# Seven-product down projection: splits of unsummed weight blocks first, two products exchanged, later transposes at a layer's end, three raw tiles before the mixer

## The chip, the cores and the metric

One core of a Trainium2 chip runs the whole program. The metric is the device time of one execution in microseconds (us), and smaller is better. TensorE is called PE here (its weight loads PEld), VectorE DVE, ScalarE ACT, GpSimd POOL, and the queue of SyncE that issues the loads of weights SP.

## The reference

Two residual layers over 256 positions and 2048 channels, all in fp32, end with an RMSNorm. Layer 0 mixes tokens with a convolution and pooling stage, layer 1 with a Fourier stage. Both layers then run the same two steps, which the change touches:

```python
x = x + square(relu(rms_norm(x) @ mlp_w1)) @ mlp_w2        # 2048 -> 8192 -> 2048
x = x + sigmoid(rms_norm(x) @ ple_w_gate) * (p @ ple_w_proj)  # 256 -> 2048
```

## The kernel before, in words

**Weights.** Every weight comes from HBM as a tile of 128 x 2048 fp32 (1 MB) into one of four `raw` buffers. Each is then split into a rounded part and a remainder, called high and low here, which go into the two halves of one of four `hl` buffers: ACT writes the high part (L110), DVE or POOL subtracts it from the raw tile to make the low part (L115). A product is three passes, high by high, high by low, low by high. `Weights.run_ahead` keeps the splits three tiles and the loads two further tiles ahead of the tile that PE takes next (`ws.next()`); a load is written down only while fewer than `RAW_BUFS` raw tiles are not yet used up.

**The mixer (`mlp`).** The 8192 hidden channels are 16 blocks of 512. `w1(q)` computes block q with four weight tiles, into two of the three PSUM buffers of `mm_pool`: first 16 matmuls with high weights (L591), then 16 narrower ones with low weights (L596). For each f from 0 to 7, `w2(f, n)` multiplies blocks 2f and 2f+1 by the weights of output columns n = 2 and n = 3 in the plain way (L356), 48 matmuls each. The columns n = 0 and 1 are computed in `pair(f)` with seven products where the plain way has eight: x is the weight tile of column block 0, y that of column block 1, each cut into halves of 1024 (at 0 and at q = 1024). Products 1, 2 and 3 take a half as it was loaded; 5, 4, 6 and 7 take sums of halves, which DVE adds in place into the raw tile (L107) before the half is split. A product is six matmuls (L668). Two such pairs of tiles, k = 0 and 1, make 14 products, and two products share one `hl` buffer, so a pair has seven such buffers, T0 to T6 below. The order of products is `SEVEN`. A prime marks a product of the second pair of tiles (4', 7').

**Gathers.** The products of a pair land in PSUM tiles a (products 1, 5), b (2, 3), c (7, 6), all from `mm_pool`, and d (4), from `sm_pool` with its two buffers. When the last product of a tile is written, `gather` adds the tile into `sums` or x on DVE (L655, L647, L649) and so frees it. After the last pair, `pair_end` combines the four parts of `sums` with x (L679).

**Order.** PE and SP run in the order in which the program is written. ACT and DVE are ordered at build time by a list scheduler that prefers what was written first; `tc.high_priority` moves work ahead. Each `tick()` counts one step of PE (six matmuls in a product), and `put_off` writes a piece of work down a number of ticks later.

**A layer's end.** When a column chunk of x is final, `Norm.chunk(c, steps)` squares it on ACT and, `steps` ticks later, transposes it on PE (eight transposes at L334 into two `sm_pool` tiles) and scales and splits it into `xT` (L273 on ACT, L278 on DVE). Chunk 2 is final before the last pair, chunks 0 and 1 after `pair_end`, chunk 3 after the last `w2`. Then `embed` computes four column blocks: a gate product with four weight tiles, one for each chunk of `xT` in the order 2, 0, 1, 3 (`ps_g`), a projection of the embedding p (`ps_e`, 12 matmuls), then sigmoid, product and sum. The embedding `pT` is loaded and split at the start of `embed`.

Of the kernel before, what the change touches and what calls it, by code (L numbers as in the profile page):

```python
# [26 lines left out]
LAYERS = 2  # L27
# [2 lines left out]
PRIO = 400  # L30
RAW_BUFS = 4

SEVEN = (1, 2, 5, 3, 6, 7, 4), (1, 5, 2, 6, 3, 4, 7)
RSQRT_MAGIC = float(0x5F3759DF)


# [8 lines left out]
class Weights:  # L45
# [4 lines left out]
    def __init__(self, nc, raw_pool, hl_pool, split_ahead, load_ahead):  # L50
        self.nc, self.raw_pool, self.hl_pool = nc, raw_pool, hl_pool
        self.split_ahead, self.load_ahead = split_ahead, load_ahead
        self.srcs, self.todo, self.raw, self.ready, self.last = [], [], {}, {}, {}
        self.loaded = self.split = self.used = 0
        self.hold = 10 ** 6

    def source(self, src, cols=2048, pieces=1):
        self.srcs.append((src, cols, pieces))
# [13 lines left out]
    def add_seven(self, tiles):  # L72

        q, parts = 1024, []
        for k, (x, y) in enumerate(tiles):
            x, y = self.source(x), self.source(y)
            made = {1: [("split", (x, 0))], 2: [("split", (x, q))], 3: [("split", (y, q))],
                    5: [("add", (x, 0), (y, 0)), ("split", (x, 0))],  # L80
                    6: [("add", (x, 0), (y, q)), ("split", (x, 0))],
                    7: [("add", (y, 0), (y, q)), ("split", (y, 0))],
                    4: [("add", (x, 0), (x, q)), ("split", (x, 0))]}
            parts += [made[p] for p in SEVEN[k]]
        for k in range(0, len(parts), 2):
            self.made([step + ((i * q, q) if step[0] == "split" else (q,))
                       for i, part in enumerate(parts[k:k + 2]) for step in part])

    def load(self, after_first=None):
        src, cols, pieces = self.srcs[self.loaded]  # L90
# [36 lines left out]
    def run_ahead(self):  # L127

        to_split = min(len(self.todo), self.used + 1 + self.split_ahead, self.hold)
        to_load = self.sources_of(min(len(self.todo), self.used + 1 + self.split_ahead + self.load_ahead) - 1)  # L130
        more = True
        while more:
            more = False
            if self.loaded < to_load and len(self.raw) < RAW_BUFS:
                self.load()
                more = True
            if self.split < to_split and self.loaded >= self.sources_of(self.split):
                self.divide()
                more = True
# [8 lines left out]
def encoder(ctx: ExitStack, tc: tile.TileContext, a, out: bass.AP):  # L148
# [60 lines left out]
    def add_ple(i):  # L209
        for n in range(4):  # L210
            parts = [(a["ple_w_gate"][i, n, c], 2048) for c in (2, 0, 1, 3)]
            parts.insert(0 if i == LAYERS - 1 and n == 3 else 4, (a["ple_w_proj"][i, n], 1024))
            for src, cols in parts:
                ws.add(src, cols=cols)

# [40 lines left out]
    def put_off(f, steps=4):  # L256

        later.append([steps, f])
# [11 lines left out]
    def divide_psum(dst, src, scale):  # L270

        hi, lo = dst
        nc.scalar.activation(hi, src, AF.Identity if scale is not None else AF.Copy,  # L273
                             scale=1.0 if scale is None else scale)
        if scale is None:
            nc.vector.tensor_tensor(lo, src, hi.bitcast(F32), ALU.subtract)
        else:
            nc.vector.scalar_tensor_tensor(lo, src, scale, hi.bitcast(F32), ALU.mult, ALU.subtract)  # L278
# [288 lines left out]
    def mlp(i, norm, after):  # L567
# [64 lines left out]
        def pair(f):  # L632


            tiles = {}

            def psum(p):

                key, half = {1: ("a", 0), 5: ("a", 1), 2: ("b", 0), 3: ("b", 1), 7: ("c", 0), 6: ("c", 1), 4: ("d", 0)}[p]
                if key not in tiles:  # L640
                    name = f"ps_s{i}_{f}{key}"
                    tiles[key] = sm_pool.tile([P, 512], F32, tag="sm", name=name) if key == "d" else psum_mm(name)
                return tiles[key][:, half * 512:(half + 1) * 512]

            def gather(p):
                if p == 3:
                    nc.vector.tensor_tensor(x[:, 0, :1024], tiles["b"], x[:, 0, :1024], ALU.add)  # L647
                elif p == 4:
                    nc.vector.tensor_tensor(x[:, 1, :512], tiles["d"], x[:, 1, :512], ALU.add)  # L649
                elif p in (5, 7):  # L650
                    ps, to = (tiles["a"], sums[:, :1024]) if p == 5 else (tiles["c"], sums[:, 1024:])
                    if f == 0:
                        nc.scalar.activation(to, ps, AF.Copy)
                    else:
                        nc.vector.tensor_tensor(to, ps, to, ALU.add)  # L655

            k = 0
            for q in (2 * f, 2 * f + 1):
                h, g = hidden[q], forms[q]
                for p in SEVEN[q % 2]:  # L660
                    if k % 2 == 0:
                        w = ws.next()
                    for kt in range(2):
                        for m, (s, j) in enumerate(PASSES_W_MOVES):
                            act = {1: h[:, s, kt, :P], 2: h[:, s, 2 + kt, :P], 4: h[:, s, 2 + kt, P:], 5: g[:, s, 0, kt],
                                   6: g[:, s, 1, kt], 7: g[:, s, 2, kt], 3: g[:, s, 3, kt]}[p]
                            col = (k % 2) * 1024 + kt * 512
                            nc.tensor.matmul(psum(p), lhsT=act, rhs=w[:, j, col:col + 512],  # L668
                                             start=q % 2 == 0 and kt == 0 and m == 0,
                                             stop=q % 2 == 1 and kt == 1 and m == 2)  # L670
                    tick()
                    k += 1
                    if q % 2:
                        gather(p)

        def pair_end():
            m1, m5, m7, m6 = (sums[:, k * 512:(k + 1) * 512] for k in range(4))
            c11, c12, c21, c22 = (x[:, t, n * 512:(n + 1) * 512] for t in range(2) for n in range(2))
            add, sub = ((lambda to, p, q, op=op: nc.vector.tensor_tensor(to, p, q, op)) for op in (ALU.add, ALU.subtract))  # L679
            add(c11, c11, m1)  # L680
            sub(m6, m6, m1)
            sub(c21, c21, m6)
            add(c21, c21, m7)
            after.chunk(0, 7)
            sub(m5, m6, m5)
            add(c12, c12, m5)
            add(c22, c22, m5)
            sub(c22, c22, m7)
            after.chunk(1, 9)

        put_off(scales, 10)
        w1(0)
        w1(1)
        for f in range(8):
            if f < 7:
                w1(2 * f + 2)
            w2(f, 2)
            if f < 7:
                w2(f, 3)
                pair(f)  # L700
                w1(2 * f + 3)
                continue
            after.chunk(2)
            pair(f)
            with tc.high_priority(offset=PRIO):
                pair_end()
            w2(f, 3)
            after.chunk(3)

    def embed(i, norm, after, gate_chunk=None, order=None):  # L710
        pt = work.tile([P, 2, S], F32, name="pt", tag="sv")
        nc.sync.dma_start(out=pt, in_=a["pT"][i])
        pT = act_pool.tile([P, 2, 2, S], F32R, tag="act", name=f"pT{i}")
        divide_psum(halves(pT), pt, None)
        for n in range(4):
            final = gate_chunk is not None and n == 3
            if final:
                pg = [psum_mm(f"ps_g{i}_{n}{k}") for k in range(3)]
                pe = [sm_pool.tile([P, 512], F32, tag="sm", name=f"ps_e{i}_{n}{t}") for t in range(2)]
                rows_product(pe, pT, range(2), True, True)  # L720
            else:
                pg = psum_mm(f"ps_g{i}_{n}")
                pe = psum_mm(f"ps_e{i}_{n}")
            if n == 3:
                ws.hold = ws.used + 7

# [22 lines left out]
            else:  # L749
                for k, c in enumerate((2, 0, 1, 3)):  # L750
                    rows_product(pg, norm.xT[c], range(4), k == 0, k == 3)
                rows_product(pe, pT, range(2), True, True)
                if order is not None and n == 3:
                    order.enter_context(in_order())
                for t in range(2):
# [4 lines left out]
                    after.chunk(n)  # L760

    nple = Norm("ple0", R_PLE)
    mlp(0, norm, nple)
    norm = Norm("od", R_OD)
    order = ctx.enter_context(ExitStack())
    embed(0, nple, norm, order=order)

# [65 lines left out]
        norm.chunk(n)  # L835

    nple = Norm("ple1", R_PLE + 16)
    mlp(1, norm, nple)
    gfin = act_pool.tile([P, D], F32, tag="act", name="gfin")
    nc.scalar.dma_start(out=gfin, in_=a["final_norm"].partition_broadcast(P))  # L840
    fin = Norm("fin", None, 5)
# [24 lines left out]
            nc.scalar.activation(c[2], c[2], AF.Copy, scale=r)  # L866
            nc.sync.dma_start(out=ov[:, t, 1024:], in_=x[:, t, 1024:])

    embed(1, nple, None, last)


def _tiles(w, k=512, n=512):
# [78 lines left out]
```

## Time and profile before

| | |
|---|---|
| median of 3 runs | 2001.64 us (2001.09 to 2003.33) |
| the profiled execution | 2001.22 us, of which the span from the first to the last instruction is 1999.4 |
| busy in the span | PE 97%, PEld 82%, DVE 78%, ACT 52%, POOL 6% |
| mean granted clock of PE | 0.993 of full speed |
| chain that ended last, by engine | PE 80%, DVE 17%, ACT 1%, issue 1% |
| mean DMA rate | 189 GB/s |
| stages by PE's timeline, in us | token mixing of layer 0: 0 to 253; mixer 253 to 938; layer end and gates to 1065; Fourier stage and its projection to 1179; mixer to 1864; layer end, gates and the last norm to 1999 |

A row of a timeline gives the start, the time, the engine, the line, the operation, what it writes and reads, the shape, the number of instructions and, in brackets, the idle time before them and who ended it. Rows of one kind that follow each other are merged into one. A later row of the same engine may start a little before the row ahead of it has ended, since instructions overlap at their ends: the distance of two starts is the pace.

### The profile page before, as it was taken

Reading aid. Unit: us, or ns where it says so; the run is one execution under the profiler, and the core shown is the slowest. Engines: PE = TensorE matmul, PEld = TensorE weight load, DVE = VectorE, ACT = ScalarE, POOL = GpSimd, SP = SyncE. Lnnn points to the kernel's source line nnn. Section 1 sums busy time; section 2 is a strip of 40 time slices with the busy share of each in tenths; the row PEclk is TensorE's granted clock in tenths of the full one; section 3 lists DMA queues with packets and bytes.
Section 4 is the critical chain, followed back from the end, with each engine's and each line's share of the span. In section 5 each row is a group of like instructions: output and inputs, shape, how many; then the busy total and the mean of one; then the engine's idle time right before and its main releaser. Section 6 shows DMA issues by size and latency. Waiting matters only on the chain.

```text
span 1999.4 us, 24088 instructions
## 1 busy us (share of the span) xinstructions
PE 1948.0 (97%) x9730; PEld 1649.4 (82%) x9730; DVE 1566.5 (78%) x1771; ACT 1041.2 (52%) x1087; POOL 128.8 (6%) x65
## 2 busy tenths in 40 slices
PE   7999999999999999999899999999999999999797
PEld 6888888888888888887789888888888888888686
DVE  7888768787978879799655557978888797888854
ACT  6445655555555455546455445555555555546543
POOL 2875000000000000000001000000000000000000
PEclk9999999999999999999899999999999999999999
DMA  8555544636546364654453555456463654645632
GB/s 340 179 179 211 190 174 163 232 136 244 188 170 232 148 236 152 242 193 161 152 180 135 194 188 186 170 194 217 161 233 137 242 192 166 232 147 190 226 140 102
DMA packets 55664, 377.43 MB, mean 189 GB/s; under 512 B 6384, under 2 KB 6528, under 8 KB 11648
## 3 DMA queue, kind: packets, MB, share of 16 engines
q1 hardware_dynamic: 55152, 374.82, 51.5%
q8 instruction: 76, 1.25, 0.2%
q10 hardware_dynamic: 144, 1.05, 0.1%
q14 instruction: 36, 0.29, 0.0%
q0 software_dynamic: 256, 0.02, 0.0%
HBM read 373.75 MB, written 2.10 MB: 188 GB/s over the span
## 4 chain that ended last, share of the span: by engine, by line
PE 80%; DVE 17%; ACT 1%; issue 1%; DMA 0%; SPq 0%; ACTq 0%
PE ps_h L591 23%; PE ps_o L356 16%; PE ps_h L596 12%; DVE hl L115 9%; PE ps_g L356 8%; PE ps_od L356 4%; DVE raw L107 4%; PE ps_in L356 4%; PE ps_out L356 3%; PE ps_pool L356 2%; ACT hl L110 1%; PE ps_outp L356 1%; PE ps_e L356 1%; DVE sums L655 1%; DVE x L377 1%
## 5 line engine op out<-in xcount | busy, mean ns | idle before, releaser
L110 ACT ACTIVATE hl<-raw 128x1024 fp32r<-128x1024 f32 (+2 forms) x529 | 775.5, 1491 | 689.2 <-PE ps_h L596 244.1
L115 DVE TENSOR_TENSOR hl<-raw,hl 128x2048 fp32r<-128x2048 f32 (+3 forms) x501 | 861.7, 1743 | 298.4 <-ACT hl L110 296.9
L591 PE MATMUL ps_h<-xT_mlp,hl 128*128 128x512 f32 x2048 | 488.2, 390 | 0.0
L591 PEld LDWEIGHTS ps_h<-xT_mlp,hl 128*128 128x128 f32 x2048 | 377.4, 188 | 73.7
L356 PE MATMUL ps_o<-hl,h 128*128 128x512 f32 x1536 | 355.2, 392 | 0.6 <-DVE hl L115 0.6
L356 PEld LDWEIGHTS ps_o<-hl,h 128*128 128x128 f32 x1536 | 288.7, 189 | 60.7 <-DVE hl L115 1.5
L596 PEld LDWEIGHTS ps_h<-xT_mlp,hl 128*128 128x128 f32 x2048 | 262.6, 191 | 9.9
L596 PE MATMUL ps_h<-xT_mlp,hl 128*128 128x256 f32 x2048 | 266.0, 283 | 0.0
L356 PE MATMUL ps_g<-hl,xT_ple 128*128 128x512 f32 (+1 forms) x816 | 179.9, 380 | 0.0
L356 PEld LDWEIGHTS ps_g<-hl,xT_ple 128*128 128x128 f32 x816 | 147.8, 190 | 28.8 <-DVE hl L115 0.4
L115 POOL TENSOR_TENSOR hl<-raw,hl 128x2048 fp32r<-128x2048 f32 (+1 forms) x28 | 120.7, 4325 | 57.3 <-ACT hl L110 57.3
L356 PE MATMUL ps_in<-hl,xT_ev 128*128 128x512 f32 x384 | 91.7, 399 | 6.3 <-ACT hl L110 6.3
L453 DVE SCALAR_TENSOR_TENSOR acc<-vp,vT,acc 128x256 f32<-128x256 f32 x240 | 96.4, 482 | 0.1
L356 PEld LDWEIGHTS ps_in<-hl,xT_ev 128*128 128x128 f32 x384 | 73.2, 192 | 23.1 <-ACT hl L110 6.7
L606 ACT ACTIVATE relu<-ps_h 128x512 f32<-128x512 f32 x64 | 38.2, 598 | 97.5 <-PE ps_h L596 97.5
L356 PE MATMUL ps_od<-hl,f 128*128 128x512 f32 x384 | 88.1, 390 | 0.0
L356 PEld LDWEIGHTS ps_od<-hl,f 128*128 128x128 f32 x384 | 71.8, 188 | 14.8
L107 DVE TENSOR_TENSOR raw<-raw,raw 128x1024 f32<-128x1024 f32 x64 | 77.9, 1218 | 0.5
L107 DVE TENSOR_TENSOR raw<-raw 128x1024 f32<-128x1024 f32 x64 | 77.7, 1217 | 0.1
L607 DVE TENSOR_TENSOR relu<-ps_h,relu 128x512 f32<-128x512 f32 x64 | 43.7, 686 | 29.8 <-ACT relu L606 29.8
L800 POOL CAST top<-z 128x4 fp32r<-128x4 f32 x8 | 1.5, 190 | 897.1 <-DVE z L278 897.1
L622 ACT ACTIVATE g<-form 128x512 fp32r<-128x512 f32 x64 | 38.4, 624 | 22.6 <-DVE form L619 11.7
(283 smaller groups left out, 1697.2 us busy)
## 6 DMA issues: line engine op xcount, KB each, us to landing
raw<-in_mlp_w SPq DMA_DIRECT2D x256, 1024.0 KB, 4.9
raw<-in_ple_w_gate SPq DMA_DIRECT2D x32, 1024.0 KB, 6.4
raw<-in_w_in SPq DMA_DIRECT2D x20, 1024.0 KB, 5.1
raw<-in_ev_w_out SPq DMA_DIRECT2D x16, 1024.0 KB, 4.8
raw<-in_od_w_out SPq DMA_DIRECT2D x16, 1024.0 KB, 4.9
raw<-in_w_in SPq DMA_DIRECT2D x16, 256.0 KB, 6.4
raw<-in_ple_w_proj SPq DMA_DIRECT2D x8, 512.0 KB, 3.6
x<-in_x SPq DMA_DIRECT2D x2, 1024.0 KB, 9.1
```

The costliest lines, as they stand in the source:

```text
L107: self.nc.vector.tensor_tensor(src, src, self.raw[other[0]][:, other[1]:other[1] + w], ALU.add)
L110: self.nc.scalar.activation(hl[:, 0, to], src, AF.Copy)
L115: getattr(self.nc, lo).tensor_tensor(hl[:, 1, to], src, hl[:, 0, to].bitcast(F32), ALU.subtract)
L356: nc.tensor.matmul(ps[t][:, cols], lhsT=acts[:, s, kt, t * P:(t + 1) * P], rhs=w[:, m, kt * 512 + cols.start:kt * 512 + cols.stop], start= ...
L377: nc.vector.tensor_tensor(xs, ps[:, t * 512:(t + 1) * 512], xs, ALU.add)
L453: nc.vector.scalar_tensor_tensor(acc, src, cwT[:, ch, k:k + 1], acc, ALU.mult, ALU.add)
L591: nc.tensor.matmul(pss[p][:, e], lhsT=w[:, 0, ch], rhs=norm.xT[c][:, :, kt], start=c == 0 and kt == 0, stop=False, skip_group_check=True)
L596: nc.tensor.matmul(pss[p][:, e, 1], lhsT=w[:, 1, ch], rhs=norm.xT[c][:, 0, kt], start=False, stop=c == 3 and kt == 3, skip_group_check=True)
L606: nc.scalar.activation(r, pss[p][:, :, 1], AF.Copy)
L607: nc.vector.tensor_tensor(s, pss[p][:, :, 0], r, ALU.add)
L622: nc.scalar.activation(g[:, 0, to], src, AF.Copy)
L655: nc.vector.tensor_tensor(to, ps, to, ALU.add)
```

## The change

The order of the second seven becomes 1, 5, 2, 6, 3, 7, 4. The sum that product 7 needs is made together with that of product 6. In each `hl` buffer the sums are now written down first, then the splits of halves that need no sum of their own step, then the others. Gathers of a pair are written down after product 6' (tile a), after 7' (tile b) and after 4' (c and d). Chunks 0, 1 and 3 at a layer's end are transposed after 10, 13 and 8 ticks (before 7, 9 and 4). The embedding is loaded and split before chunk 2 and the last pair, and the first of the four projections of p stands ahead of its gate product, in the list of weights too. Until the mixer of layer 0 begins, three raw tiles may be in use rather than four.

```diff
-SEVEN = (1, 2, 5, 3, 6, 7, 4), (1, 5, 2, 6, 3, 4, 7)
+SEVEN = (1, 2, 5, 3, 6, 7, 4), (1, 5, 2, 6, 3, 7, 4)
...
+        self.raws = RAW_BUFS - 1
...
-            made = {1: [("split", (x, 0))], 2: [("split", (x, q))], 3: [("split", (y, q))],
-                    5: [("add", (x, 0), (y, 0)), ("split", (x, 0))],
-                    6: [("add", (x, 0), (y, q)), ("split", (x, 0))],
-                    7: [("add", (y, 0), (y, q)), ("split", (y, 0))],
-                    4: [("add", (x, 0), (x, q)), ("split", (x, 0))]}
-            parts += [made[p] for p in SEVEN[k]]
+            made = {1: ((x, 0), []), 2: ((x, q), []), 3: ((y, q), []), 5: ((x, 0), [((x, 0), (y, 0))]),
+                    6: ((x, 0), [((y, 0), (y, q)), ((x, 0), (y, q))]), 7: ((y, 0), []), 4: ((x, 0), [((x, 0), (x, q))])}
+            parts += [(p, *made[p]) for p in SEVEN[k]]
         for k in range(0, len(parts), 2):
-            self.made([step + ((i * q, q) if step[0] == "split" else (q,))
-                       for i, part in enumerate(parts[k:k + 2]) for step in part])
+            two = list(enumerate(parts[k:k + 2]))
+            adds = [("add", to, by, q) for _, (_, _, sums) in two for to, by in sums]
+            two.sort(key=lambda part: (len(part[1][2]) > 0, part[0]))
+            self.made(adds + [("split", src, i * q, q) for i, (_, src, _) in two])
...
-            if self.loaded < to_load and len(self.raw) < RAW_BUFS:
+            if self.loaded < to_load and len(self.raw) < self.raws:
...
-            parts.insert(0 if i == LAYERS - 1 and n == 3 else 4, (a["ple_w_proj"][i, n], 1024))
+            parts.insert(0 if n == 0 or i == LAYERS - 1 and n == 3 else 4, (a["ple_w_proj"][i, n], 1024))
...
-                    if q % 2:
-                        gather(p)
+                    if q % 2 and p in (6, 7, 4):
+                        for done in {6: (5,), 7: (3,), 4: (7, 4)}[p]:
+                            gather(done)
...
-            after.chunk(0, 7)
+            after.chunk(0, 10)
...
-            after.chunk(1, 9)
+            after.chunk(1, 13)
 
         put_off(scales, 10)
+        ws.raws = RAW_BUFS
...
+            pT = embedding(i)
             after.chunk(2)
             pair(f)
...
             w2(f, 3)
-            after.chunk(3)
+            after.chunk(3, 8)
+        return pT
...
                 pg = psum_mm(f"ps_g{i}_{n}")
                 pe = psum_mm(f"ps_e{i}_{n}")
+                if n == 0:
+                    rows_product(pe, pT, range(2), True, True)
...
-                rows_product(pe, pT, range(2), True, True)
+                if n:
+                    rows_product(pe, pT, range(2), True, True)
```

`embedding(i)` holds the four lines that stood at the start of `embed`: the DMA of p, the tile `pT`, and its split.

## Rows read from the trace of the kernel before

**Rows 1.** Stretches: length, busy PE, PEld, DVE, ACT, POOL (instructions), PEclk, DMA share, GB/s.
```profile
916.00:938.00 22.00, 20.71 (x94) 16.62 (x94) 22.00 (x23) 15.09 (x18) 0.00 (x0) 1.00 0.34 116
...
950.00:970.00 20.00, 14.10 (x56) 11.69 (x57) 14.72 (x33) 10.13 (x22) 0.00 (x0) 0.74 0.44 158
...
938.00:985.00 47.00, 39.28 (x166) 31.87 (x166) 34.10 (x48) 21.81 (x32) 0.00 (x0) 0.89 0.53 197
...
1864.00:1912.00 48.00, 38.77 (x170) 30.96 (x170) 34.51 (x48) 22.01 (x32) 0.00 (x0) 0.93 0.58 218
```

**Rows 2.** Who waited for whom, PE: us in total, times, longest.
```profile
PE tr_ple L334 <- DVE x L679: 9.9, 2, 5.0
...
PE ps_s_7d L668 <- DVE xT_ple L278: 2.4, 2, 1.2
PE ps_s_5d L668 <- DVE hl L115: 1.5, 2, 0.8
```

**Rows 3.** Timeline of PE in the pair of f = 1, layer 0.
```profile
429.57 1.52 PE L668 MATMUL ps_s_1a<-hl,h 128*128 128x512 f32 x6
...
444.53 1.52 PE L668 MATMUL ps_s_1b<-hl,g 128*128 128x512 f32 x6
446.03 0.49 PE L668 MATMUL ps_s_1d<-hl,h 128*128 128x512 f32 x1
447.28 1.45 PE L668 MATMUL ps_s_1d<-hl,h 128*128 128x512 f32 x5 [0.76 <-DVE hl L115]
...
449.95 2.43 PE L591 MATMUL ps_h<-xT_mlp,hl 128*128 128x512 f32 x10
```

**Rows 4.** Timeline of DVE in the same pair.
```profile
439.04 1.22 DVE L107 TENSOR_TENSOR raw<-raw,raw 128x1024 f32<-128x1024 f32 x1
441.38 2.36 DVE L115 TENSOR_TENSOR hl<-raw,hl 128x1024 fp32r<-128x1024 f32 x2 [1.12 <-ACT hl L110]
443.66 1.22 DVE L107 TENSOR_TENSOR raw<-raw 128x1024 f32<-128x1024 f32 x1
444.80 1.22 DVE L655 TENSOR_TENSOR sums<-ps_s_1a,sums 128x1024 f32<-128x1024 f32 x1
446.01 1.22 DVE L115 TENSOR_TENSOR hl<-raw,hl 128x1024 fp32r<-128x1024 f32 x1
447.15 1.22 DVE L647 TENSOR_TENSOR x<-ps_s_1b,x 128x1024 f32<-128x1024 f32 x1
448.28 4.48 DVE L115 TENSOR_TENSOR hl<-raw,hl 128x2048 fp32r<-128x2048 f32 x2
```

**Rows 5.** Timeline of ACT in the same pair.
```profile
440.29 2.01 ACT L110 ACTIVATE hl<-raw 128x1024 fp32r<-128x1024 f32 x2 [3.67 <-DVE raw L107]
...
445.88 3.70 ACT L110 ACTIVATE hl<-raw 128x2048 fp32r<-128x2048 f32 x2
```

**Rows 6.** Timeline of PE, last pair and layer end of layer 0, then of layer 1.
```profile
916.27 1.52 PE L668 MATMUL ps_s_7a<-hl,h 128*128 128x512 f32 x6
...
921.72 1.03 PE L334 MATMUL tr_ple<-ident,x 128*128 128x128 f32 x8
922.50 2.99 PE L668 MATMUL ps_s_7c<-hl,g 128*128 128x512 f32 x12
...
938.06 0.39 PE L356 MATMUL ps_o<-hl,h 128*128 128x512 f32 x1
...
985.85 2.88 PE L356 MATMUL ps_e<-hl,pT 128*128 128x512 f32 x12
...
1864.28 0.39 PE L356 MATMUL ps_o<-hl,h 128*128 128x512 f32 x1
...
1912.10 2.88 PE L356 MATMUL ps_e<-hl,pT 128*128 128x512 f32 x12
```

**Rows 7.** Timeline of DVE at the same layer end of layer 0.
```profile
952.71 2.61 DVE L679 TENSOR_TENSOR x<-x,sums 128x512 f32<-128x512 f32 x4
...
955.88 0.69 DVE L276 TENSOR_TENSOR pT<-pt,pT 128x512 fp32r<-128x512 f32 x1
```

More of the change, by code (lines that the diff above doesn't have):

```diff
@@ L707, in mlp, with embedding @@
             w2(f, 3)
-            after.chunk(3)
-    def embed(i, norm, after, gate_chunk=None, order=None):
+            after.chunk(3, 8)
+        return pT
+    def embedding(i):
         pt = work.tile([P, 2, S], F32, name="pt", tag="sv")
@@ L714, in embed @@
         divide_psum(halves(pT), pt, None)
+        return pT
+    def embed(i, pT, norm, after, gate_chunk=None, order=None):
         for n in range(4):
@@ L762, in encoder @@
     nple = Norm("ple0", R_PLE)
-    mlp(0, norm, nple)
+    pT = mlp(0, norm, nple)
     norm = Norm("od", R_OD)
     order = ctx.enter_context(ExitStack())
-    embed(0, nple, norm, order=order)
+    embed(0, pT, nple, norm, order=order)
     dft = ws.next()
@@ L837, in encoder @@
     nple = Norm("ple1", R_PLE + 16)
-    mlp(1, norm, nple)
+    pT = mlp(1, norm, nple)
     gfin = act_pool.tile([P, D], F32, tag="act", name="gfin")
@@ L867, in last @@
             nc.sync.dma_start(out=ov[:, t, 1024:], in_=x[:, t, 1024:])
-    embed(1, nple, None, last)
+    embed(1, pT, nple, None, last)
 def _tiles(w, k=512, n=512):
```

## The prediction

> **What bounds the kernel now.** I read the page's busy times first, then the stretches, the chain of waits, PE's waits, and the timelines of PE, DVE and ACT in one pair of the mixer and at both layer ends. PE has work 97% of the span, so what can be won is what PE loses, and its losses have two places.
>
> The first is the end of every pair. Products follow each other at (444.53 - 429.57) / 11 = 1.36 us, and 14 of them take 19.04. From the first matmul of the pair to the first of the next `w1` the trace has 449.95 - 429.57 = 20.38 [rows 3], so a pair loses 1.34. The reader should see the gap inside product 4': its first matmul needs only the high part, the second stands until the low part is there [rows 3]. On DVE, that low part (446.01) comes last in a chain: the sum for 6' at 439.04, idle for 1.12 while ACT makes the high part of 6' (440.29, right after that sum), lows of 6' and 7', the sum for 4', gather a while ACT makes the high part of 4', and only then the low of 4', which ends at 447.23 [rows 4, 5]. PE goes on at 447.28. The same wait stands once in each of the seven pairs f = 0 to 6 of both layers, 14 in all: the row of one f counts two [rows 2].
>
> The second is the end of a layer. From the end of the last pair to the projection of the first gate block PE takes 985.85 - 938.06 = 47.79 us, in layer 1 1912.10 - 1864.28 = 47.82 [rows 6]. Its work there is 48 matmuls of `w2`, 96 of the gate and three groups of eight transposes: 144 / 6 x 1.36 + 3 x 0.78 = 34.98, with 922.50 - 921.72 = 0.78 for a group [rows 6]. So each layer end loses 12.8. Some 5.0 of that is the first transpose waiting for `pair_end` [rows 2]; after it the granted clock is 0.74 from 950 to 970 and 0.89 and 0.93 over the whole layer ends [rows 1], which means that PE ran part of the stretch at the lower of its two levels, 1.2 instead of 2.4 GHz. One late sum is paid for twice.
>
> **Order of sums and splits, and the exchange of 4' and 7'.** The count of DVE and ACT instructions stays: eight sums and 14 splits in a pair. Only places change. The sum for 7' moves ahead of that for 6', the low of 3' comes behind the sum for 6', so DVE has work while ACT makes the high part of 6': 1.12 saved. The low of 7' does the same while ACT makes that of 4'. Gather a is written down later, behind product 6', so it need not stand ahead of the low of 4': another 1.14 (446.01 - 444.80 is 1.21, the other steps 1.14 [rows 4]). The low of 4' then ends near 447.23 - 2.26 = 445.0. PE wants 7' at 429.57 + 12 x 1.36 = 445.89 and 4' at 447.25. Margin 2.3: the wait goes wholly, 14 x 1.34 = 18.8. Bounds: nothing won, and 18.8.
>
> What is late next is the gather of tile b. It is now written behind product 7', and so behind the splits of the three tiles that come next, which cost DVE 4.48 / 2 = 2.24 each [rows 4]. The next `w1` begins at 429.57 + 19.04 = 448.6 in the one free PSUM buffer and wants a second after eight matmuls of 1.36 / 6, at 450.4. Tile b is complete at 445.9. If the gather runs when it is ready, or behind one split (446.1 + 2.24 + 1.22 = 449.6), nothing waits. I take that: before, the gather at 447.15 ran ahead of the next splits (448.28) [rows 4], although two of the three were written ahead of it. The other outcomes are rivals below.
>
> **The last pair of a layer** takes 938.06 - 916.27 = 21.79 against 19.04 + 0.78, a loss of 1.97, of which 1.2 is product 4 waiting for a buffer that chunk 2's transposes hold [rows 2, 6]. These are not moved. The split of the embedding now falls into this stretch, in which DVE is busy 22.00 of 22 [rows 1]; it costs DVE 0.69 [rows 7], and better order may give 0.8 back. I take 0, with 0.7 either way. The load of the embedding moves forward on SP, past the loads for the last `w2`. Those wait for raw buffers that only this pair's own splits free, while the embedding waits for a buffer that the last `w1` has read before the pair starts; so nothing behind it on SP is held, cost 0. If that cover failed, the last `w2` would get its tile late and the layer end would pay the same way it pays now.
>
> **The layer's end.** Before, x for chunk 0 is there at 952.71 + 0.68 = 953.4, 15.3 after the pair's end [rows 7, 6]. On that way DVE makes the lows of three gate tiles of 2.24; after, the first of the three is the projection's, half as wide: 1.1 less, so 14.2. The transposes come after eight steps of `w2` and two of the projection, 10 x 1.36 = 13.6 after the pair's end, where they came after 7 x 1.36 = 9.5. That leaves 0.6, with the embedding's 0.7 upstream at most 1.3. PE meets xT of chunk 0 four gate steps plus a group later, 6.2, for four scalings. Chunks 1 and 3 keep at least three steps (4.1) of distance to the group ahead. No operation is added; the projection's 12 matmuls (2.72) are moved. Of the 12.8 I keep 3.0 as lost, for the 1.3, a late first low and what the scalings may still hold up: 2 x 9.8 = 19.6. Bounds: 0, and 2 x 12.8 = 25.6.
>
> At the gate block n = 0 the projection no longer stands between gate product and sigmoid. In layer 0 the next norm's transposes follow four steps (5.4) later, enough for two sigmoids and four DVE steps; if not, at most the lost cover of 2.7. I take 0.
>
> **Three raw tiles.** Until the mixer, sources are one tile each, and loads run two tiles ahead of splits, so a load is written down with at most two in use: the lower limit never binds, and the four buffers stay. Cost 0; if it did bind, one load would be written one split later, still ahead of its use.
>
> **Sum.** 18.8 + 19.6 = 38.4. Against the profiled execution's own 2001.22 us (span 1999.4 plus 1.8 around it; the median is 2001.64, 0.02% more) that gives 1962.8, say 1963. All losses gone, 18.8 + 2 x (12.8 + 2.0) = 48.4, give 1953.
>
> **The rivals.** *Two splits ahead of gather b.* If ACT is earlier too, lows of two tiles are ready first: the gather ends at 446.1 + 4.48 + 1.22 = 451.8, PE stands for 1.4 where it stood for 1.34, and the pair gains nothing: 2001.2 - 19.6 = 1982. For it: those two tiles are written ahead of the gather, and their high parts followed directly on that of 4' [rows 5], which is now earlier. Against it: the order in the trace before. 0.18.
>
> *Three splits ahead: slower.* The gather ends at 454.0, PE stands for 3.6, 2.3 more than before, 14 times: 2001.2 + 32 - 19.6 = 2014. It decides from the point at which the gather ends 2.7 after 450.4, where 14 x (2.7 - 1.34) eats the layer ends. Against it: the third tile's raw buffer is freed by the pair's own last splits. 0.13. The Trainium skill, "TensorE: Matmul & The Clock Gate", in its table of specifications, calls VectorE's queue a strict FIFO; by that, a gather that stands behind ready splits cannot pass them. No run here shows an overtaking either.
>
> *The layer end pays nothing*, because another wait takes the place (tile a's gather late and the last `w2` without a PSUM buffer, or scalings late): 2001.2 - 18.8 = 1982. For it: DVE is full there [rows 1]. 0.11.
>
> *Buffers, not order, hold the pair.* The four `hl` buffers could be what spaces the splits; then reordering leaves the 1.34: 2001.2 - 19.6 = 1982. Against it: DVE idles for ACT, and ACT for a sum on DVE [rows 4, 5], not for a buffer. 0.05. The Trainium skill, "Perfetto Trace Analysis", section "Optimization Strategy", reads the same gap repeating on the engine that should be saturated as a possible lack of SBUF or PSUM for the next tile; by that rule this rival would be the likeliest, and the row of the releaser speaks against it.
>
> *Nothing moves*, because the list scheduler had already found this order, or gains and stalls cancel: 2001. 0.07.
>
> **How the numbers follow.** Forecast 0.46, with 1953 to 1973 as its own range (layer ends 7 to 12.8 each, pairs 1.0 to 1.34). With the three cases near 1982, and 6 for their layer ends falling short, 1953 to 1988 holds 0.80; what is left out is 0.13 above and 0.07 at no change. About 0.2% is what a measurement of this kernel can tell from no change. Faster: 0.46 + 0.18 + 0.11 + 0.05 = 0.80; same 0.07; slower 0.13.
>
> **What would show it.** The pair: no gap in product 4', the next `w1` 19.0 to 19.1 after the pair's start, no idle of DVE at 6', and gather b ahead of 2.24-wide lows or behind one. If a gap appears eight matmuls into `w1`, the gather is late. The layer end: no wait of the first transposes above 1.5, granted clock near 1.00 through it, 36 to 39 us instead of 47.8. Up to the mixer, timelines unchanged. The prediction is wrong if PE waits for PSUM at the start of `w1` or of the last `w2`, or if the clock still falls at the layer ends.

## The result, and the profile after

The changed kernel takes 2024.43 us in the median of four runs (2022.2 to 2026.49), the kernel before, beside it, 2002.1 (2001.09 to 2003.33): 1.0111 times as long, with an interval of 1.0094 to 1.0129. The forecast was 1963 with a range of 1953 to 1988. It was wrong in direction; what came is near the rival "three splits ahead" (2014), but only in the total: that rival has 32 us lost in the pairs and 19.6 won at the layer ends, where about 25 were lost and 2.4 won. One execution of a later run (5029.57 us) lies far from its companions, for a reason that no run shows, and is left out of every ratio. The profiled spans are 2020.4 and 1999.4, so 21.0 us are to be found. Line numbers here are those of the changed kernel: up to `pair` they are two higher than before (`w1` L593, products L670, sums L109, high L112, low L117, gather a or c L657, b L649, d L651).

From the starts of the pairs and of the next norm's transposes, and from the end of the last matmul, in PE's timelines:

| part | forecast | measured |
|---|---|---|
| up to the first pair | 0 | 341.49 against 342.91: -1.4 (up to there the other runs below lie between 341.1 and 344.0, so this is chance) |
| step of the pair f = 0, twice | -1.34 each | 426.82 - 341.49 = 85.33 against 86.66: -1.33 each |
| steps of the pairs f = 1 to 6, twice | -1.34 each | 604.40 - 515.62 = 88.78 against 86.63: +2.15 each, 25.8 in all; one of them 1.6 more |
| last pair, layer 0 and 1 | 0 | 26.37 and 26.73 against 21.79 and 21.78: +4.6 and +4.95 |
| from there to the next norm, or the end | -9.8 each | 50.45 against 55.95: -5.5; 118.62 against 125.01: -6.4 |

These sum to 20.9. The last two rows together are what the layer ends gave: 2.4 us where 19.6 was forecast.

Who waited for whom on PE: in total, times, longest.

```profile
PE ps_h L593 <- DVE x L649: 28.6, 12, 2.4
PE ps_s_7d L670 <- DVE xT_ple L280: 7.7, 2, 4.4
...
PE tr_ple L336 <- DVE rstd_ple L286: 3.1, 2, 1.6
PE tr_ple L336 <- DVE xT_ple L280: 3.1, 2, 1.6
...
PE ps_s_1d L670 <- DVE hl L117: 1.0, 2, 0.5
```

The first row is new: twelve times the first `w1` tile stands for gather b. The wait for tile d has grown from 1.2 each to 3.3 and 4.4, the 5.0 of the first transposes [rows 2] is gone, and product 4' still waits, 0.5 in place of 0.8.

The pair of f = 1 on PE, from the start of 4':

```profile
444.50 0.39 PE L670 MATMUL ps_s_1d<-hl,h 128*128 128x512 f32 x1
445.41 1.43 PE L670 MATMUL ps_s_1d<-hl,h 128*128 128x512 f32 x5 [0.51 <-DVE hl L117]
446.67 1.98 PE L593 MATMUL ps_h<-xT_mlp,hl 128*128 128x512 f32 x8
451.04 2.08 PE L593 MATMUL ps_h<-xT_mlp,hl 128*128 128x512 f32 x8 [2.39 <-DVE x L649]
```

The same pair on DVE, then on ACT:

```profile
436.17 1.22 DVE L109 TENSOR_TENSOR raw<-raw,raw 128x1024 f32<-128x1024 f32 x1
437.31 2.44 DVE L117 TENSOR_TENSOR hl<-raw,hl 128x1024 fp32r<-128x1024 f32 x2
439.67 1.22 DVE L657 TENSOR_TENSOR sums<-ps_s_1a,sums 128x1024 f32<-128x1024 f32 x1
440.80 1.22 DVE L109 TENSOR_TENSOR raw<-raw 128x1024 f32<-128x1024 f32 x1
441.93 7.82 DVE L117 TENSOR_TENSOR hl<-raw,hl 128x2048 fp32r<-128x2048 f32 x4
449.67 1.22 DVE L649 TENSOR_TENSOR x<-ps_s_1b,x 128x1024 f32<-128x1024 f32 x1
```

```profile
437.43 2.87 ACT L112 ACTIVATE hl<-raw 128x1024 fp32r<-128x1024 f32 x2 [1.13 <-DVE raw L109]
440.67 4.71 ACT L112 ACTIVATE hl<-raw 128x2048 fp32r<-128x2048 f32 x3 [0.38 <-ACT hl L112]
```

The 1.12 of DVE idle in [rows 4] is filled, and PE leaves the pair 19.85 after its start (446.67 - 426.82) instead of 20.38 [rows 3]. But the row at 441.93 holds four low parts: that of 4' and three 2.24 us wide ones of the next tiles, 3 x 2.24 + 1.14 = 7.86. Gather b, whose tile PE had complete at about 443.3, just after 7' began, starts at 449.67, and `w1` loses 451.04 - 446.67 - 8 x 1.36 / 6 = 2.56.

Last pair and layer end on PE, layer 0:

```profile
932.66 3.00 PE L670 MATMUL ps_s_7c<-hl,g 128*128 128x512 f32 x12
938.92 1.62 PE L670 MATMUL ps_s_7d<-hl,h 128*128 128x512 f32 x6 [3.26 <-DVE xT_ple L280]
...
949.46 0.49 PE L670 MATMUL ps_s_7d<-hl,h 128*128 128x512 f32 x1 [0.74 <-ACT hl L112]
950.77 2.22 PE L670 MATMUL ps_s_7d<-hl,h 128*128 128x512 f32 x5 [0.82 <-DVE hl L117]
952.79 11.92 PE L358 MATMUL ps_o<-hl,h 128*128 128x512 f32 x48
...
973.98 0.63 PE L336 MATMUL tr_ple<-ident,x 128*128 128x128 f32 x4 [1.56 <-DVE rstd_ple L286]
```

The last pair of layer 0, that of layer 1, and the stretch after the pair in layer 0 (columns as in [rows 1]):

```profile
926.42:952.79 26.37, 21.54 (x93) 16.98 (x92) 26.11 (x26) 15.97 (x19) 0.00 (x0) 0.97 0.47 164
...
1864.89:1891.62 26.73, 22.33 (x94) 18.03 (x93) 25.20 (x26) 15.86 (x19) 0.00 (x0) 0.87 0.47 163
...
952.79:999.79 47.00, 42.93 (x190) 35.09 (x189) 32.56 (x48) 24.17 (x34) 0.00 (x0) 0.94 0.50 188
```

DVE is busy for 26.11 of the 26.37 us of the pair in layer 0, and for 25.20 of 26.73 in layer 1. Part of the added time is not waiting: in the kernel before, PE was busy for 20.50 and 20.48 us in these pairs at a granted clock of 1.00, here for 21.54 and 22.33 at 0.97 and 0.87. In the 47 us after the pair of layer 0, PE is at 0.94 of its clock where it had 0.89 [rows 1].

### The profile page after: what moved, and what is told of

Its sections match the earlier page's. It is cut to its first block, busy times and chain, and to the rows that moved or that the text cites. A ratio compares the mean times of both kernels' runs of the same rounds, so it can differ in the third digit from the quotient of the medians.

```text
span 2020.4 us, 24088 instructions
## 1 busy us (share of the span) xinstructions
PE 1947.5 (96%) x9730; PEld 1650.4 (82%) x9730; DVE 1564.6 (77%) x1771; ACT 1043.6 (52%) x1087; POOL 128.8 (6%) x65
## 4 chain that ended last, share of the span: by engine, by line
PE 78%; DVE 17%; issue 3%; ACT 1%; DMA 1%; SPq 0%; ACTq 0%; DVEq 0%
PE ps_h L593 22%; PE ps_o L358 16%; PE ps_h L598 12%; DVE hl L117 10%; PE ps_g L358 8%; PE ps_od L358 4%; PE ps_in L358 4%; DVE raw L109 3%; PE ps_out L358 3%; PE ps_pool L358 2%; PE ps_outp L358 1%; PE ps_e L358 1%; DVE x L649 1%; DVE x L379 1%; PE ps_f L371 1%
## 5 line engine op out<-in xcount | busy, mean ns | idle before, releaser
L112 ACT ACTIVATE hl<-raw 128x2048 fp32r<-128x2048 f32 (+2 forms) x529 | 778.3, 1493 | 716.9 <-PE ps_h L598 281.1
L117 DVE TENSOR_TENSOR hl<-raw,hl 128x2048 fp32r<-128x2048 f32 (+3 forms) x501 | 863.2, 1745 | 325.4 <-ACT hl L112 324.0
L593 PE MATMUL ps_h<-xT_mlp,hl 128*128 128x512 f32 x2048 | 493.2, 392 | 28.6 <-DVE x L649 28.6
L593 PEld LDWEIGHTS ps_h<-xT_mlp,hl 128*128 128x128 f32 x2048 | 377.5, 189 | 106.8 <-issue 33.3
L117 POOL TENSOR_TENSOR hl<-raw,hl 128x2048 fp32r<-128x2048 f32 (+1 forms) x28 | 120.7, 4325 | 55.9 <-ACT hl L112 55.9
L109 DVE TENSOR_TENSOR raw<-raw 128x1024 f32<-128x1024 f32 x64 | 78.1, 1220 | 0.6
L109 DVE TENSOR_TENSOR raw<-raw,raw 128x1024 f32<-128x1024 f32 x64 | 78.1, 1220 | 0.0
```

Source lines behind the costliest of these rows:

```text
L109: self.nc.vector.tensor_tensor(src, src, self.raw[other[0]][:, other[1]:other[1] + w], ALU.add)
L112: self.nc.scalar.activation(hl[:, 0, to], src, AF.Copy)
L117: getattr(self.nc, lo).tensor_tensor(hl[:, 1, to], src, hl[:, 0, to].bitcast(F32), ALU.subtract)
L593: nc.tensor.matmul(pss[p][:, e], lhsT=w[:, 0, ch], rhs=norm.xT[c][:, :, kt], start=c == 0 and kt == 0, stop=False, skip_group_check=True)
```

## The experiments

Two theories for the pairs stood against each other. Mine: neither the order of sums and splits nor the late gathers costs anything alone; the new order makes the next tiles' splits ready ahead of a gather that is written down late. Rivals: the late gathers cost by themselves, or the new order does.

**Old places of the gathers, in the changed kernel.**

```diff
-                    if q % 2 and p in (6, 7, 4):
-                        for done in {6: (5,), 7: (3,), 4: (7, 4)}[p]:
-                            gather(done)
+                    if q % 2:
+                        gather(p)
```

> The changed kernel, with each gather of a pair written down right behind its own product again. In the changed kernel PE stands 2.39 us eight matmuls into the next w1, 12 times, for the gather of tile b, which DVE runs behind three splits of 2.24 us. Theory 1 (writing the gathers later is what put the third split ahead): with the old places the third split comes behind the gather, the gather ends about 2.2 us earlier, the stand shrinks to 0.2 us, and the time falls by 12 x 2.2 = 26 us from 2024 to about 1998. Rival (the new order of sums and splits brings the next tiles' splits forward whatever the place of the gathers): the stand stays, 2020 to 2025 us.

Measured 1991.17, ratio to before 0.9946 (0.9931 to 0.9961): 33 us less than the change, where 26 were expected. The pair takes 19.87, and the gap in `w1` has shrunk to under 0.4: its first tile takes 3.99 us, 3.63 before. DVE runs gather b one wide split earlier, behind 4' and two of them:

```profile
441.77 5.62 DVE L117 TENSOR_TENSOR hl<-raw,hl 128x2048 fp32r<-128x2048 f32 x3
447.31 1.22 DVE L649 TENSOR_TENSOR x<-ps_s_1b,x 128x1024 f32<-128x1024 f32 x1
```

**Only gather b put back.** `{6: (5,), 3: (3,), 4: (7, 4)}` in place of `{6: (5,), 7: (3,), 4: (7, 4)}`.

> The changed kernel with one gather put back: that of tile b is written down behind product 3' again, the others stay late. If the loss is gather b standing behind three splits (theory), one split less stands ahead of it, the 2.4 us wait of w1 for PSUM tile ps_h goes, and the time falls by the whole of what the four gathers together gave, from 2024 to 1990 to 1994. Rival, the late places of gathers a, c and d cost as well (a standing ahead of the sum for 4' or the next pair's tiles): it stays above 2003.

1987.56, 0.9931 (0.9915 to 0.9948): gather b alone carries the loss.

**Late gathers alone, in the kernel before,** behind 6', 4' and 7' there.

> The kernel before, with only the gathers of a pair written down later (tile a behind product 6', b behind 4', c and d behind 7', the same number of products later as in the change). Theory 1 as a cause of its own (late gathers are run late): the gather of tile b falls behind splits of 2.24 us and PE stands at the start of w1, at least 14 x 1 us more, 2015 us or above. Theory 2 (it takes both: only where the chain of sums and splits ends earlier are the next splits ready ahead of the gather): 2000 to 2004 us, no change.

2001.02, 0.9999 (0.9989 to 1.0009): in the old order the late places cost nothing.

**Order of sums and splits alone,** with the exchange of 4' and 7', gathers and layer end as before.

> The kernel before, with only the new order of sums and splits in a pair and products 4' and 7' exchanged; gathers right behind their products, layer ends as before. The prediction gave this 14 x 1.34 = 18.8 us of gain, 1983 us. Theory from the changed kernel's trace: the gather of tile a and the 2.24 us split of the next tile take the place that was won, the wait in product 4' goes from 1.34 to 0.91 us and a stand of about 0.2 us appears in w1: a gain of 14 x 0.2 to 0.4, 1995 to 1999 us, less what the last pairs lose (up to 2 x 5 us if their loss comes from this part).

1994.37, 0.9966 (0.9954 to 0.9977), the pair 19.84. So it takes both edits: late gathers cost 0 in the old order and 33 us in the new. The last pairs take 23.99 and 25.60 here, against 21.79 and 21.78 before: the order alone lengthens them.

**The next tiles behind product 4'.** Added to the kernel with the old gathers; edges of issue order only:

```diff
+                if any(k < n <= k + 3 for k in self.ends):   # ends: each pair's last buffer
+                    for new, old in zip((hi, low), self.behind):
+                        self.tc.add_manual_dep(new.ins, old.ins.name, ...NoSync...)
+                elif n in self.ends:
+                    self.behind = hi, low
```

> The kernel with the old gathers (1991.2) with one thing added: the splits of the three tiles after a pair's last buffer are queued behind the high part (on ACT) and the low part (on DVE) of product 4', by edges of issue order alone. Theory: the remaining loss of 0.8 in a pair is the low part of 4' standing behind a 2.24 us split of the next tile; the pair takes 19.0 to 19.1, no wait for hl within it, 14 x 0.8 = 11 us less, and the last pairs lose up to 2.4 each less: 1975 to 1981. Rival: the next tiles' splits, now later, make the following w1 wait (for hl or ps_h) as much as was won: pair 19.04 but a gap in w1, 1988 to 1994.

1975.53 in the median of three executions, 0.9873 (0.9856 to 0.9889); the 1976.4 of later expectations is the median of all four. PE and DVE in the pair of f = 1 (products L679, sums L111, low L119, gathers L666 and L658, `w1` L602 here):

```profile
428.59 1.52 PE L679 MATMUL ps_s_1a<-hl,h 128*128 128x512 f32 x6
...
446.27 1.52 PE L679 MATMUL ps_s_1d<-hl,h 128*128 128x512 f32 x6
447.63 3.79 PE L602 MATMUL ps_h<-xT_mlp,hl 128*128 128x512 f32 x16
```

```profile
441.43 1.22 DVE L666 TENSOR_TENSOR sums<-ps_s_1a,sums 128x1024 f32<-128x1024 f32 x1
442.56 1.22 DVE L111 TENSOR_TENSOR raw<-raw 128x1024 f32<-128x1024 f32 x1
444.90 1.23 DVE L119 TENSOR_TENSOR hl<-raw,hl 128x1024 fp32r<-128x1024 f32 x1 [1.13 <-ACT hl L114]
446.05 1.22 DVE L658 TENSOR_TENSOR x<-ps_s_1b,x 128x1024 f32<-128x1024 f32 x1
447.18 6.69 DVE L119 TENSOR_TENSOR hl<-raw,hl 128x2048 fp32r<-128x2048 f32 x3
```

447.63 - 428.59 = 19.04: the pair loses nothing, with the same buffers, and with gather a still ahead of the sum for 4'. The last pairs, which were to lose less too, take 27.29 and 26.96.

**The layer end alone,** in the kernel before: transposes later, embedding ahead of the last pair, first projection ahead of its gate product.

> The kernel before, with only the part of the change at a layer's end: later transposes, embedding split before the last pair, first projection ahead of its gate product. The prediction gave this part 2 x 9.8 = 19.6 us of gain, which is 1982 us. In the changed kernel the layer ends are 5.6 and 6.5 us shorter but the last pairs 4.6 and 4.9 us longer. If the last pair grows because of this part (the embedding's split in a stretch where DVE is full): 1997 to 2001 us. If it grows because of the order of sums and splits: 1988 to 1992 us.

1990.17, 0.9944 (0.9929 to 0.9958). In layer 0 the last pair grows from 21.79 to 23.68, what follows to the next norm's transposes falls from 55.95 to 49.44. In layer 1 the pair grows from 21.78 to 26.44. The time lies where it was expected if only the order lengthened the last pair, but the pairs say otherwise: the layer-end part lengthens it too.

That left the last pair. Six runs tried its order, all with the old gathers.

**Chunk 2 first:** transposed after three steps instead of four, its scalings at high priority.

> The kernel with the old gathers (1991.2) with one thing added: chunk 2 is transposed one product earlier (3 steps instead of 4) and its four scalings and four lows stand ahead of ready splits (high priority). Theory: product 4 of the last pair waits 3.26 for a buffer because the lows of chunk 2 stand behind sums and splits that the new order makes ready earlier; the wait goes, and with it the half clock after it: the last pair falls from 29.7 to 22 to 24, so 2 x 6 to 2 x 8 us, total 1976 to 1980. Rival 1, the splits put back by these eight instructions make a later product wait instead: last pair 26 or more, 1985 to 1991. Rival 2, the half clock does not come from this wait and stays.

1985.75, 0.9923 (0.9908 to 0.9937). The wait for tile d is gone, but the pair still takes 26.56: waits of 1.6, 0.7, 1.8 and 1.2 for `hl` stand in its place (rival 1).

**Chunk 2 first and the next tiles behind 4', together.**

> Both additions: chunk 2 first and the next tiles behind product 4'. If each does what the theory says and they do not share a cause: 1991.2 - 11 (pairs) - 2 x 7 to 2 x 10 (last pairs 20 to 22) = 1960 to 1966, granted clock near 1 at both layer ends. If the last pair is held by DVE's work and not by its order: last pair 24 or more, 1972 to 1980.

1974.52, 0.9865 (0.9851 to 0.988): no less than with the next tiles behind 4' alone, as far as the intervals tell. The last pairs take 24.04 and 25.43.

**Split of the embedding behind `pair_end`,** first in the layer end alone, then with the next tiles behind 4':

> The layer-end part alone (1990.2, last pair 23.7 where the kernel before has 21.8) with one thing changed: the embedding is loaded ahead of the last pair as there, but split behind pair_end. Theory: my step that took the last pair at nothing failed because DVE is full there, and the split of the embedding (0.7 on DVE, ahead of chunk 2's lows) pushes them back: the last pair returns to 21.8 to 22.4 and the time falls by 2 x 1.3 to 2 x 1.9, to 1986 to 1988. Rival: the split costs the same wherever it stands, and the layer end gives back what the pair wins: 1989 to 1991.

> The kernel with the next tiles behind product 4' (1976.4), with the split of the embedding behind pair_end. Theory as above: the wait for tile d (3.3 and 4.4 now) falls by about the split and what it pushed, 1 to 2 us in each layer, 1972 to 1974.5. Rival, the order of sums alone makes the wait: it stays above 3 and the time at 1976.

1992.17, 0.9953 (0.9938 to 0.9968), and 1973.46, 0.9859 (0.9842 to 0.9875). The edit writes the split down later, but in DVE's timeline it stands behind the last pair only in layer 0 of the first run (at 945.52, the pair ends at 938.16). There the pair is back at 21.80, so the split was what lengthened it. In layer 1 the split still runs at 1847.18, ahead of the second half of chunk 2's lows, and the pair takes 26.10 with a wait for tile d of 3.3; the time does not fall. In the second run it stays within both pairs (925.81 and 1829.58); the wait for tile d is 2.66 instead of 3.27 in layer 0, where the split now comes after it, and still 4.4 in layer 1, and the time is 2 us less than without this edit, with intervals that overlap.

**Chunk 2 behind the last pair** (18 steps), with the above.

> The same, and chunk 2 is transposed and scaled behind the last pair (18 steps instead of 4), so nothing of the layer's end stands in the last pair. Theory: the last pair's loss is the work of the layer's end that shares DVE and the two small PSUM buffers with it; without it the pair takes 19.0 to 20.5 instead of 27, the transposes add 0.8 to the layer end, total 1976.4 - 2 x 5 to 2 x 7 = 1962 to 1967. Rival: DVE is as full at the layer end, so the first gate product waits for chunk 2 and the layer end grows by as much as the pair shrinks: 1972 to 1978.

1972.96, 0.9859 (0.9845 to 0.9874): the pair falls to 22.22 and the stretch after it grows to 51.42 (47.69 without this edit). The rival held.

**All these edits of order** (next tiles behind 4', chunk 2 first, embedding's split late).

> All edits of order together: next tiles behind product 4', chunk 2 transposed after 3 steps and scaled first, split of the embedding behind pair_end. If order is what the last pair lacks, it takes 19.8 to 21 (24.0 without the late embedding) and the time is 1968 to 1971. If VectorE is full there, another wait for hl stays or comes, last pair 22.5 to 25, 1972 to 1975.

1972.91, 0.9856 (0.9841 to 0.987), as was expected if DVE is full. Last pair, what follows, and both:

```profile
905.73:929.88 24.15, 20.81 (x93) 16.44 (x92) 22.80 (x25) 14.61 (x19) 0.00 (x0) 1.00 0.36 115
929.88:978.35 48.47, 44.39 (x206) 35.95 (x204) 39.23 (x52) 28.28 (x40) 0.00 (x0) 1.00 0.62 225
905.73:978.35 72.62, 65.20 (x298) 52.38 (x296) 62.04 (x76) 42.89 (x58) 0.00 (x0) 1.00 0.54 188
```

The order is not used up, though. One wait of PE in this pair, and what DVE did before it ended:

```profile
924.53 1.42 PE L683 MATMUL ps_s_7c<-hl,g 128*128 128x512 f32 x5 [1.81 <-DVE hl L119]
```

```profile
919.26 0.68 DVE L287 TENSOR_TENSOR pT<-pt,pT 128x512 fp32r<-128x512 f32 x1
...
922.13 1.22 DVE L670 TENSOR_TENSOR sums<-ps_s_7a,sums 128x1024 f32<-128x1024 f32 x1
923.26 1.22 DVE L119 TENSOR_TENSOR hl<-raw,hl 128x1024 fp32r<-128x1024 f32 x1
```

The embedding's split is still inside the pair, gather a stands right ahead of the low part that PE waits for, and DVE is busy for 22.80 of 24.15 us.

**Part of it on GpSimd:** the low parts of the last pair's fifth buffer, of the first projection tile and of the first gate tile.

> The same, and GpSimd makes four low parts that VectorE makes there: both of the last pair's fifth buffer (5' and 2', 2.4 us each on GpSimd by its row in the trace before, 1.14 on VectorE) and those of the first projection tile and of the first gate tile. If VectorE is full, the last pair falls to 19.8 to 21.5 and the waits of the transposes shrink: 1962 to 1968. Rival: GpSimd's slower low parts come late themselves, product 5' or the first gate waits for GpSimd, and nothing is won: 1972 to 1978.

1985.07, 0.9914 (0.9897 to 0.993): slower than either case expected, for a reason that I had not weighed (last section). This run does not tell whether DVE is full.

**Half of the last pair's low parts left out.** All edits of order, and:

```diff
+                if lo == "half":                              # buffers of the pair f = 7 only
+                    on, to, src = "vector", slice(other, other + w // 2), self.raw[r][:, c:c + w // 2]
...
-                            col = (k % 2) * 1024 + kt * 512
+                            col = (k % 2) * 1024 + (0 if f == 7 and j == 1 else kt * 512)
```

> The kernel with all edits of order (1972.9, last pairs 24.15 and 24.10). In the last pair of a layer VectorE makes only half of each low part (128x512 for 128x1024), and the second half of each product's low pass reads the first half again: the pair's low parts are left out by half, PE, ACT and the transfers have the same work. A 128x512 low part takes 0.54 us less than one of 128x1024 by the rows of the trace before (0.68 and 1.22), 14 times 7.6 us. If VectorE's amount of work is what the last pair lacks, its four waits (1.5, 1.8, 1.2 and 1.9, 1.3, 1.2) go, the pair takes 19.8 to 20.5, and the time falls by 2 x 4 to 2 x 6, to 1961 to 1965. If the chain of sums, high parts and low parts or the order holds it, waits of 3 or more in all stay and the time is 1968 to 1973.

1960.04, 0.9794 (0.9777 to 0.981). Last pair, the stretch to the end of gate block 0, and pair plus all up to the next norm's transposes:

```profile
905.77:925.72 19.95, 19.95 (x94) 16.59 (x93) 19.28 (x24) 15.90 (x20) 0.00 (x0) 1.00 0.52 177
925.72:965.60 39.88, 38.18 (x181) 31.60 (x180) 31.37 (x46) 22.32 (x31) 0.00 (x0) 1.00 0.61 222
905.77:971.15 65.38, 63.68 (x297) 52.73 (x296) 55.17 (x74) 42.62 (x58) 0.00 (x0) 1.00 0.58 206
```

In layer 0 the pair has no wait left, PE is at its full clock, and pair plus end fall from 72.62 to 65.38: 7.2 us, while DVE's busy time in them falls by 6.9, from 62.04 to 55.17. The stretch after the pair, in which no low part is halved, gives 3.0 of that (48.47 to 45.43). In layer 1 the pair falls from 24.10 to 20.33. So time on DVE is what the last pair lacked, and what it leaves undone there is paid for behind it. This run does not rule order out: a halved low part also shortens the way from a sum to its low part, and no run tried the new order with both the embedding's split and gather a behind the low parts that PE waits for.

## Why the prediction was wrong, step by step

**The first order of the pair: right in part.** The idle at 6' went, as said. But "it need not stand ahead of the low of 4': another 1.14" was wrong twice: gather a stands ahead still, and it was not what binds. What now keeps 4' late is ACT, which makes the high part of a next tile ahead of that of 4', and DVE, which makes a next tile's low part first. The step promised 14 x 1.34; with the old gathers a step took 86.53 against 86.63 wherever gathers are on DVE, because most of the 0.5 won in the pair came back in the first `w1` tile (3.99 us instead of 3.63). That is the prediction's rival "two splits ahead of gather b". With the next tiles queued behind 4' the pair won the whole 1.34, and a step took 85.33.

**"I take that": the step that failed.** I let gather b run when ready or behind one split, because the trace of before showed it ahead of the next splits. There it was ahead for want of others: DVE was a chain to 4', and no next tile's high part was ready. The change takes that away and writes the gather later. It came behind three splits, 2.15 more a step, twelve times, not the 2.3 of the rival fourteen times: at f = 0 gathers a and c are on ACT, the pair takes 19.04 and wins its 1.33. The argument against the rival, that the third tile's raw buffer is freed by the pair's own last splits, was true of the load and did not hold the split. The trace agrees with what the Trainium skill, "TensorE: Matmul & The Clock Gate", states of VectorE's queue in its table of specifications (a strict FIFO): gather b, whose tile was complete at about 443.3, starts when the four low parts ahead of it are done.

**"Buffers, not order".** The stalled PE does now wait for a PSUM tile, and the Trainium skill, "Perfetto Trace Analysis", section "Optimization Strategy", says that a gap that repeats on the engine that should be saturated can mean too little SBUF or PSUM. With the same buffers and only edges of order the gap is 0, so here it did not mean that, and the row of the releaser decided rightly.

**"The last pair: I take 0, with 0.7 either way".** It cost 4.6 and 4.95. I had seen DVE busy for 22.00 of 22 us and still priced an added split and a changed order at nothing. Each of them alone lengthens the pair: the layer-end part by 1.9 and 4.7, the order by 2.2 and 3.8. In layer 0 the split of 0.7 cost 1.9, since without it the pair is back at 21.80. A clock term was missing as well: PE's busy time in the pair rose by 1.0 and 1.85 at the lower granted clock.

**"Of the 12.8 I keep 3.0 as lost: 2 x 9.8".** The transposes' long wait went as said, but 5.5 and 6.4 came, of which the pair took 4.6 and 4.95 back. From the start of the last `w2` to the end of gate block 0 the work of PE is 34.98 + 2.72 = 37.7. The run with half of the low parts takes 39.88 in layer 0, a loss of 2.2: the step's own mechanism was sized well for a DVE with room, which it did not have behind the last pair. Pair and layer end have 61.0 us of DVE work before and 62.04 with all edits of order, against about 63 of PE's (77.74 less the 1.97 and 12.8 lost).

**Raw tiles, the embedding's load, the gates: right.** Up to 250 us the traces of before (four raw tiles) and after (three) have the same instructions in the same order on every engine, and none of the waits listed above is for a load or at the first projection.

What stays open: why the scheduler, in the new order, takes all three splits ahead of gather b rather than one or two was not tried; that they are ready first by its own reckoning is argued from the rows. Nor was gather a moved by itself. Whether another order of the last pair could do without its waits was not shown either.

## What to carry to other kernels

An instruction that runs early in a trace may do so only because nothing else was ready; before you write it later, or make others ready earlier, ask what would then be queued ahead of it, and fix the order with an edge if PE waits for it. In a stretch in which an engine is busy for all of it, take no edit for free: price each added instruction at least in full, and look at that engine's sum over the stretch beside the work of PE. A gain at one wait is real only once the pieces on both sides of it are measured together.

## What the runs showed of the hardware that was not expected

**DVE's sums of two SBUF tiles stand still while GpSimd splits.** In the run with GpSimd, its low part of the first gate tile, and DVE beside it:

```profile
937.81 5.06 POOL L120 TENSOR_TENSOR hl<-raw,hl 128x2048 fp32r<-128x2048 f32 x1
```

```profile
935.49 1.22 DVE L672 TENSOR_TENSOR sums<-ps_s_7c,sums 128x1024 f32<-128x1024 f32 x1
936.62 0.68 DVE L666 TENSOR_TENSOR x<-ps_s_7d,x 128x512 f32<-128x512 f32 x1
937.22 1.18 DVE L696 TENSOR_TENSOR sums<-sums 128x512 f32<-128x512 f32 x1
938.43 4.99 DVE L696 TENSOR_TENSOR x<-x,sums 128x512 f32<-128x512 f32 x1
```

A sum of two SBUF tiles that takes 0.68 elsewhere takes 4.99 and ends 0.55 after GpSimd's instruction; two of the pair's sums take 3.39 and 2.62 instead of 1.22 in the same way. The gathers, which read one operand from PSUM, keep 1.22 and 0.68 while GpSimd works (its instruction before the one shown began at 933.94). The Trainium skill, "SBUF — State Buffer", section "Who interferes with whom", says that VectorE instructions with two SBUF inputs contend with GpSimd instructions that read SBUF, and that whoever issues first holds the shared ports for its whole instruction while the other blocks; these rows agree with it.

**The clock does not fall after every wait of the same length.** The products behind the wait for tile d, with the old gathers and with only gather b put back:

```profile
925.20 2.90 PE L670 MATMUL ps_s_7d<-hl,h 128*128 128x512 f32 x6 [3.26 <-DVE xT_ple L280]
927.90 2.76 PE L670 MATMUL ps_s_7a<-hl,h 128*128 128x512 f32 x6
```

```profile
927.86 1.63 PE L670 MATMUL ps_s_7d<-hl,h 128*128 128x512 f32 x6 [3.27 <-DVE xT_ple L280]
929.32 1.53 PE L670 MATMUL ps_s_7a<-hl,h 128*128 128x512 f32 x6
```

After 3.26 us six matmuls take 2.7, the pace of 1.2 GHz (granted clock 0.50 from 927.90 to 930.40); after 3.27 us they keep 1.36 to 1.46, that of 2.4 GHz (granted clock 1.00 from 927.80 to 932.00). The last pair takes 29.73 in the first and 25.61 in the second, in one execution each, so a single profile can misjudge this stretch by 4 us.
